# A two-layer float32 encoder on one core: projections in three 256-column products, twelve unread products at the start, and two rearranged hand-overs

## The chip, the cores and the metric

The kernel runs on one core of a Trainium2 chip. The metric is the device time of one execution in microseconds (us); smaller is better. Engines are named as the profile names them: PE (TensorE's products), PEld (its weight loads), ACT (ScalarE), DVE (VectorE), POOL (GpSimd), SP (SyncE, which issues most transfers). "L247" is line 247 of the kernel before.

## The reference, cut to what matters

```python
D_MODEL, SEQ, DEPTH, HEAD_DIM = 2048, 256, 2, 128      # one sequence of 256 tokens
N_MIX_HEADS, N_KV_HEADS, N_MEM_HEADS, N_MEM, D_FF = 12, 4, 4, 256, 8192

def reference(x, mem, ...):
    m = rms_norm(mem, mem_norm)
    h = x
    for i in range(DEPTH):
        n = rms_norm(h, attn_norm[i])
        if i == 0:      # neighbourhood attention with a bias
            q, k, v, qm = split(n @ a_w_in, [1536, 3072, 4608])
            mix = neighbourhood_attention(q, k, v, a_rpb)
        else:           # grouped-query attention, normed and rotated q and k
            q, k, v, qm = split(n @ b_w_in, [1536, 2048, 2560])
            mix = gqa_block_attention(rope(norm(q)), rope(norm(k)), v)
        km, vm = split(m @ w_mem_kv[i], 2)
        cross = memory_attention(qm, km, vm)               # 4 heads into 256 memory tokens
        h = h + concatenate([mix, cross]) @ w_o[i]
        n = rms_norm(h, mlp_norm[i])
        h = h + square(relu(n @ w_up[i])) @ w_down[i]
    return rms_norm(h, final_norm)
```

All inputs and the output are float32.

## The kernel before, in words

Every matrix is multiplied in split form: `split` (L327 to L330) makes from a float32 tile a rounded high part on ACT (L329) and the remainder, its low part, on DVE (L330). A product is then high x high, high x low and low x high, each one PE instruction, all added into one accumulator (PSUM has eight banks). Weights come from memory in chunks of 128x2048 (`raw`, 1 MB), are split in two halves of 1024 columns, and each half is one *grain* of PE work.

There are three kinds of chunk:

- **S chunks** (`s_products`, L240): one head of a projection whose result is wanted with features on partitions: `w_km0`, `w_km1`, `w_aqm` (4 chunks each), `w_aq`, `w_ak` (12 each), 36 in all, each over 16 steps of the inner dimension. The weights are stationary and the activations (`memT` or `nT`, 512 columns: 256 of high part, 256 of low part) move. A step is one product of 512 columns with the high weights (L247) and one of 256 columns with the low weights (L250), issued as two wide ones, then two narrow ones (`GROUP`). The bank holds two sums of 256 columns; `summed` (L368) adds them: a copy on ACT (L371), an addition on DVE (L373) and, for all callers, a multiplication by a row on DVE (L375).
- **M chunks** (`m_products`, L226): activations stationary, weights moving, 512 columns each, at L234, L237 and L238.
- **U chunks** (`up_grains`, `u_products`, L727): the MLP's first matrix. Weights are stationary, and a step is three products of 256 columns into one sum: high weights with both parts (L735), low weights with the high part (L736). The MLP's second matrix is done with seven accumulators `p1` to `p7` (L849 to L851).

In `begin` (L253) the first three S chunks are multiplied while the memory `memT` and their weights arrive in pieces of 256 KB; SP issues these, except the first piece of each of the three weights, which ACT issues (L142).

After that, `run_all` (L283) goes through a list of grains. Ahead of each grain it emits the load (8 grains ahead), an optional middle stage, and the split of later grains (4 ahead in the MLP); after it, a clock called `tick` goes on by one and starts what `later(n, ...)` has put off. A planner then orders the instructions of each engine by simulated times; `past` (L638) and `pin` keep instructions behind given ones.

Three places matter besides the S chunks:

- **The beginning of the MLP.** The last block of the output projection ends (`o_done`, `nb == 3`), its result is transposed into `hT`, and the first U chunks run. The split halves of U chunks are in `uh` and `ul`, two buffers each (`half_of_side`, L738), so the fourth half, grain (0, 1, 1), waits for the buffers of the second. The last block's own addition to `h`, its squares and `inv` are put off by 8, 10 and 12 ticks behind the transposes (L702 to L706).
- **The last query block's heads.** `b_q_done(blk)` starts four attention heads at ticks 1, 3, 5 and 7; each has its scores, its transposes and its values' product 3 ticks apart, and in block 2 the last of these is another tick later (`rest`). Their outputs are read by the output projection right behind.
- **The accumulators.** `sum_of` (L868) takes the seven banks of the MLP in the order p4, p3, p1, p2, p5, p7, p6.

Places in SBUF count in this program by their byte address modulo 256. In U chunks the moving data stand at 160 and the weights at 224, 64 further, but for the last step's high part, which stands at 128 (96 from the weights). In S chunks, in M chunks and in attention, both operands of a product stand at the same place.

Of the kernel before, what the change touches and what calls it, by code (L numbers as in the profile page):

```python
# [17 lines left out]
P = 128  # L18
# [17 lines left out]
GROUP = 2  # L36
# [6 lines left out]
MOVING_AT = 160  # L43

# [46 lines left out]
def encoder_kernel(ctx: ExitStack, tc: tile.TileContext, t: dict, out: bass.AP):  # L91
# [44 lines left out]
    for j in range(8):  # L136
        s = slice(j * 512, (j + 1) * 512)
        nc.sync.dma_start(mem0[:, s], t["memT"][:, s])
        if j % 2 == 0:
            s = slice(j * 256, (j + 2) * 256)  # L140
            for c in range(FIRST_CHUNKS):
                (nc.sync if j else nc.scalar).dma_start(raws[c][:, s], t["w_km0"][c][:, s])  # L142
# [11 lines left out]
    nc.scalar.activation(warm, mhalf[:, :1], AF.Exp)  # L154

# [10 lines left out]
    def halves_of(w):  # L166
# [9 lines left out]
        def prep(hf):  # L176
# [7 lines left out]
            tiles[hf] = new_half()  # L184
# [24 lines left out]
    def new_half():  # L209
        return (at.ring.tile([P, HALF], F32R, tag="hi", bufs=4, name="hi"),  # L210
                at.ring.tile([P, HALF], F32R, tag="lo", bufs=4, name="lo"))
# [28 lines left out]
    def s_products(w, k0, nk, hi, lo):  # L240

        acts, ps = w.acts(), w.ps
        for j0 in range(0, nk, GROUP):
            js = range(j0, min(j0 + GROUP, nk))
            for j in js:
                s = slice(j * P, (j + 1) * P)
                nc.tensor.matmul(ps, hi[:, s], acts[:, k0 + j, :], start=k0 + j == 0, stop=False)  # L247
            for j in js:
                s = slice(j * P, (j + 1) * P)
                nc.tensor.matmul(ps[:, SEQ:], lo[:, s], acts[:, k0 + j, :SEQ], start=False,  # L250
                                     stop=k0 + j == KT - 1)

    def begin():  # L253
# [5 lines left out]
        for q in range(4):  # L259
            for k in range(4 * q, 4 * q + 4):  # L260
                split_pair(box["memT"], mem0[:, k * SEQ : (k + 1) * SEQ], G_MEM, k)
                if k % 4 == 0:
                    for c, w in enumerate(plan[:FIRST_CHUNKS]):
                        if q % 2 == 0:
                            tiles[c] = new_half()
# [33 lines left out]
    def add_s(src, acts, done):  # L299
        def start(w):  # L300
            w.ps = at.acc.tile([P, 512], F32, tag="acc", name="ps_s")
# [66 lines left out]
    def summed(ps, name, row=None, factor=1.0):  # L368

        a = at.work.tile([P, SEQ], F32, tag="sum_a", name=f"{name}_a")  # L370
        nc.scalar.activation(a, ps[:, SEQ:], AF.Copy)  # L371
        s = at.work.tile([P, SEQ], F32, tag="sum_s", name=f"{name}_s")
        nc.vector.tensor_tensor(s, ps[:, :SEQ], a, op=ALU.add)  # L373
        if row is not None:
            nc.vector.scalar_tensor_tensor(s, s, factor, row, op0=ALU.mult, op1=ALU.mult)  # L375
# [47 lines left out]
    def attention(jobs, at, gap=1, lag=1, rest=0):  # L423

# [12 lines left out]
        for t in range(len(jobs) + 2):  # L437
            for n in range(3):
                if 0 <= t - n < len(jobs):
                    j = t - n  # L440
                    more = rest if n == 2 and j == len(jobs) - 1 else 0
                    later(at + gap * j + lag * n + more,
# [838 lines left out]
```

## Time and profile before

| | us |
|---|---|
| three runs | 2047.66, 2050.84, 2047.76 |
| median | 2047.76 |
| the profiled execution, its own time | 2048.19 |
| span of the profiled execution | 2046.4 |
| PE busy in it | 2026.7 (99%) |
| DVE busy | 1667.0 (81%) |
| ACT busy | 1251.6 (61%) |
| PE's share of the chain that ended last | 93% |

The span is from the first to the last instruction; 1.8 us of the profiled execution lie outside it. PE is busy nearly all the time, and it has 93% of the chain of waits that ended last, so the time is PE's time plus what PE waits at the start, at hand-overs and at the end. Products overlap, so the spacing from one start to the next says more than the duration of one.

### The profile page before, as it was taken

The page shows a single profiled execution, that of the slowest core. Times are in us where ns is not written, and L with a number is a line of the kernel's source. Part 1 is how long each engine was busy: PE and PEld are TensorE (multiplying, and loading weights), DVE is VectorE, ACT ScalarE, POOL GpSimd, SP SyncE. Part 2 cuts the span into 40 slices and gives each one's busy share as a digit, 9 for nine tenths or more (in the row PEclk, how much of TensorE's full clock was granted, in tenths as well). Part 3 has the DMA queues.
Part 4 walks back from the last instruction along what each step waited for, and adds up shares of the span by engine and source line. Part 5 has one row for each costly group of instructions (what it writes and reads, how often), then busy time and mean ns, then how long its engine had stood idle before and what let it go on. Part 6 is the DMA issues. An engine that isn't in the chain of part 4 may idle for free.

```text
span 2046.4 us, 31582 instructions
## 1 busy us (share of the span) xinstructions
PE 2026.7 (99%) x12516; PEld 1813.8 (89%) x12516; DVE 1667.0 (81%) x2061; ACT 1251.6 (61%) x1652; POOL 119.2 (6%) x144
## 2 busy tenths in 40 slices
PE   8999999999999999999999999999999999999998
PEld 7888888889999999999988888889999999999996
DVE  6767667558989989999897667657998989999996
ACT  6755555556666666666656557556666666666664
POOL 0000000000000000000000001000000000000000
PEclk9999999999999999999999999999999999999999
DMA  7755554727777777787775554536877777777773
GB/s 281 283 190 179 191 177 169 277 80 233 231 231 232 220 232 230 226 242 222 230 222 199 180 185 144 184 125 216 246 227 227 227 231 229 234 232 227 236 221 130
DMA packets 93429, 433.79 MB, mean 212 GB/s; under 512 B 10464, under 2 KB 12128, under 8 KB 60128
## 3 DMA queue, kind: packets, MB, share of 16 engines
q1 hardware_dynamic: 75456, 398.47, 57.3%
q0 software_dynamic: 16816, 31.46, 8.7%
q8 instruction: 98, 1.61, 0.3%
q10 hardware_dynamic: 1008, 1.84, 0.3%
q14 instruction: 51, 0.42, 0.1%
HBM read 398.17 MB, written 4.19 MB: 197 GB/s over the span
## 4 chain that ended last, share of the span: by engine, by line
PE 93%; DVE 3%; DMA 2%; issue 1%; ACT 0%; POOLq 0%; POOL 0%; SPq 0%; DVEq 0%; ACTq 0%
PE ps_u L735 21%; PE ps_u L736 11%; PE ps_m L234 8%; PE ps_m L237 8%; PE ps_m L238 8%; PE p L849 8%; PE p L850 8%; PE p L851 8%; PE ps_s L247 7%; PE ps_s L250 3%; DMA t<-in_w_pair 1%; DVE tl L330 1%; PE pt_a L410 1%; DVE ul L330 1%; PE pt_n L347 1%
## 5 line engine op out<-in xcount | busy, mean ns | idle before, releaser
L735 PE MATMUL ps_u<-hT,uh 128*128 128x256 f32 x4096 | 713.2, 278 | 0.2
L735 PEld LDWEIGHTS ps_u<-hT,uh 128*128 128x128 f32 x4096 | 627.4, 188 | 10.3 <-ACT uh L329 0.6
L736 PE MATMUL ps_u<-hT,ul 128*128 128x256 f32 x2048 | 568.9, 278 | 1.6 <-DVE ul L330 1.5
L329 ACT ACTIVATE uh<-raw_U 128x1024 fp32r<-128x1024 f32 x278 | 294.6, 1061 | 307.1 <-PE ps_u L735 290.0
L330 DVE TENSOR_TENSOR lo<-raw,hi 128x1024 fp32r<-128x1024 f32 (+1 forms) x220 | 261.4, 1194 | 164.5 <-ACT hi L329 162.9
L736 PEld LDWEIGHTS ps_u<-hT,ul 128*128 128x128 f32 x2048 | 386.2, 189 | 4.2 <-DVE ul L330 3.2
L330 DVE TENSOR_TENSOR ul<-raw_U,uh 128x1024 fp32r<-128x1024 f32 x278 | 337.3, 1218 | 40.6 <-ACT uh L329 40.5
L329 ACT ACTIVATE hi<-raw 128x1024 fp32r<-128x1024 f32 (+1 forms) x220 | 227.5, 1039 | 210.2 <-PE ps_m L238 119.1
L329 ACT ACTIVATE th<-t 128x2048 fp32r<-128x2048 f32 x112 | 215.2, 1921 | 118.7 <-PE p L851 107.8
L330 DVE TENSOR_TENSOR tl<-t,th 128x2048 fp32r<-128x2048 f32 x112 | 256.0, 2286 | 23.9 <-ACT th L329 23.5
L330 DVE TENSOR_TENSOR bl<-b,bh 128x1536 fp32r<-128x1536 f32 x112 | 196.0, 1750 | 0.3 <-ACT bh L329 0.3
L850 PE MATMUL p<-tl,a_s 128*128 128x512 f32 x448 | 174.8, 390 | 0.0
L851 PE MATMUL p<-th,a_s 128*128 128x512 f32 x448 | 174.3, 389 | 0.0
L329 ACT ACTIVATE bh<-b 128x1536 fp32r<-128x1536 f32 x112 | 166.2, 1484 | 7.3 <-PE p L851 1.2
L829 POOL DMA_DIRECT2D t<-b x112 | 97.0, 866 | 1158.8 <-DVE t L828 556.0
L849 PE MATMUL p<-th,a_s 128*128 128x512 f32 x448 | 164.1, 391 | 0.0
L247 PE MATMUL ps_s<-nT,hi 128*128 128x512 f32 x448 | 142.5, 397 | 0.0
L851 PE MATMUL p<-bh,a_s 128*128 128x512 f32 x336 | 131.1, 390 | 0.0
L850 PE MATMUL p<-bl,a_s 128*128 128x512 f32 x336 | 131.0, 390 | 0.0
L828 DVE TENSOR_TENSOR t<-t,b 128x512 f32<-128x512 f32 x112 | 77.2, 689 | 57.6 <-DMA t<-in_w_pair 46.5
L849 PE MATMUL p<-bh,a_s 128*128 128x512 f32 x336 | 108.0, 389 | 0.0
L237 PE MATMUL ps_m<-lo,nT 128*128 128x512 f32 x264 | 103.7, 393 | 0.0
(237 smaller groups left out, 3305.1 us busy)
## 6 DMA issues: line engine op xcount, KB each, us to landing
raw_U<-in_w_up SPq DMA_DIRECT2D x128, 1024.0 KB, 6.6
b<-in_w_pair SPq DMA_DIRECT2D x112, 768.0 KB, 4.5
raw<-in_w_o SPq DMA_DIRECT2D x32, 1024.0 KB, 5.0
t<-in_w_pair SPq DMA_DIRECT2D x112, 256.0 KB, 3.4
t<-b POOLq DMA_DIRECT2D x112, 256.0 KB, 6.9
raw<-in_w_b SPq DMA_DIRECT2D x21, 1024.0 KB, 4.9
raw<-in_w_av SPq DMA_DIRECT2D x12, 1024.0 KB, 4.9
raw<-in_w_aq SPq DMA_DIRECT2D x12, 1024.0 KB, 4.9
```

The lines of the kernel that those rows point to most:

```text
L234: first = nc.tensor.matmul(w.ps[i], ah, hi[:, s], start=st, stop=False)
L237: nc.tensor.matmul(w.ps[i], ah, lo[:, s], start=False, stop=False)
L238: nc.tensor.matmul(w.ps[i], al, hi[:, s], start=False, stop=sp)
L247: nc.tensor.matmul(ps, hi[:, s], acts[:, k0 + j, :], start=k0 + j == 0, stop=False)
L329: first = nc.scalar.activation(dst_hi, src, AF.Copy)
L330: return first, nc.vector.tensor_tensor(dst_lo, src, dst_hi.bitcast(F32), op=ALU.subtract)
L735: nc.tensor.matmul(ps, hi[:, s], acts[:, k, x], start=k == n == 0, stop=False)
L736: nc.tensor.matmul(ps, lo[:, s], acts[:, k, :SEQ], start=False, stop=k == KT - 1)
L829: nc.gpsimd.dma_start(s[:, 0, :], block(1), accum_op=ALU.add)
L849: nc.tensor.matmul(ps, a[:, 0, ai, :], hi[:, s], start=begins, stop=False)
L850: nc.tensor.matmul(ps, a[:, 0, ai, :], lo[:, s], start=False, stop=False)
L851: nc.tensor.matmul(ps, a[:, 1, ai, :], hi[:, s], start=False, stop=ends)
```

## The change

Five edits:

1. S chunks are multiplied as U chunks are, by one helper, `products`: each step is three products of 256 columns into one sum of 256 columns (48 products in a chunk where there were 32). The last step takes the low part first. `summed` becomes one multiplication that reads the accumulator. The split halves of S chunks start 64 bytes into buffers that are 256 bytes longer; those of M chunks stay at the start. The fourth S chunk shares the third's bank.
2. Twelve products of a 128x128 tile of ones with itself, read by nobody, stand ahead of everything on PE, and SP issues all pieces of the beginning.
3. At the MLP's beginning, grain (0, 1, 1) is split into two buffers of the tag `b` (else loads of the second matrix); the last block's addition, squares and `inv` come at ticks 6, 12 and 14, each behind the split that was traced last.
4. The seven accumulators are taken in the order p4, p7, p6, p3, p1, p2, p5.
5. In block 2 the heads start at ticks 1, 3, 4 and 6, and the last values' product is no longer put off (it comes at tick 12, where it came at 14).

The diff, cut to its core:

```diff
+STILL_AT = 64
...
-                (nc.sync if j else nc.scalar).dma_start(raws[c][:, s], t["w_km0"][c][:, s])
+                nc.sync.dma_start(raws[c][:, s], t["w_km0"][c][:, s])
...
+    idle = at.att.tile([P, P], F32, tag="att", name="idle")
+    for _ in range(12):
+        nc.tensor.matmul(idle, ones, ones, start=True, stop=True)
...
-    def new_half():
-        return (at.ring.tile([P, HALF], F32R, tag="hi", bufs=4, name="hi"),
-                at.ring.tile([P, HALF], F32R, tag="lo", bufs=4, name="lo"))
+    def new_half(kind):
+        s = slice(STILL_AT // 4, STILL_AT // 4 + HALF) if kind == "S" else slice(0, HALF)
+        return tuple(at.ring.tile([P, HALF + 64], F32R, tag=n, bufs=4, name=n)[:, s] for n in ("hi", "lo"))
...
-        acts, ps = w.acts(), w.ps
-        for j0 in range(0, nk, GROUP):
-            js = range(j0, min(j0 + GROUP, nk))
-            for j in js:
-                s = slice(j * P, (j + 1) * P)
-                nc.tensor.matmul(ps, hi[:, s], acts[:, k0 + j, :], start=k0 + j == 0, stop=False)
-            for j in js:
-                s = slice(j * P, (j + 1) * P)
-                nc.tensor.matmul(ps[:, SEQ:], lo[:, s], acts[:, k0 + j, :SEQ], start=False,
-                                     stop=k0 + j == KT - 1)
+        products(w.ps, w.acts(), k0, nk, hi, lo)
+
+    def products(ps, acts, k0, nk, hi, lo):
+
+        for j in range(nk):
+            k = k0 + j
+            s = slice(j * P, (j + 1) * P)
+            parts = (slice(0, SEQ), slice(SEQ, 512))
+            for n, x in enumerate(parts if k < KT - 1 else parts[::-1]):
+                nc.tensor.matmul(ps, hi[:, s], acts[:, k, x], start=k == n == 0, stop=False)
+            nc.tensor.matmul(ps, lo[:, s], acts[:, k, :SEQ], start=False, stop=k == KT - 1)
...
-    def add_s(src, acts, done):
+    def add_s(src, acts, done, place=None):
+
         def start(w):
-            w.ps = at.acc.tile([P, 512], F32, tag="acc", name="ps_s")
+            if place != 1:
+                box["ps_s"] = at.acc.tile([P, 512], F32, tag="acc", name="ps_s")
+            w.ps = box["ps_s"][:, (place or 0) * SEQ :][:, :SEQ]
...
-    def summed(ps, name, row=None, factor=1.0):
-
-        a = at.work.tile([P, SEQ], F32, tag="sum_a", name=f"{name}_a")
-        nc.scalar.activation(a, ps[:, SEQ:], AF.Copy)
+    def summed(ps, name, row, factor=1.0):
+
         s = at.work.tile([P, SEQ], F32, tag="sum_s", name=f"{name}_s")
-        nc.vector.tensor_tensor(s, ps[:, :SEQ], a, op=ALU.add)
-        if row is not None:
-            nc.vector.scalar_tensor_tensor(s, s, factor, row, op0=ALU.mult, op1=ALU.mult)
+        nc.vector.scalar_tensor_tensor(s, ps, factor, row, op0=ALU.mult, op1=ALU.mult)
         return s
...
-                later(8, past, add)
-                later(10, past, squares)
-                later(12, past, inv)
+                for n, fn in ((6, add), (12, squares), (14, inv)):
+                    later(n, lambda fn=fn: past(fn, box["splits"][-1]))
...
         def prep(hf):
-            own[hf] = half_of_side(own["raw"], hf)
+            if (part, m, hf) == (0, 1, 1):
+
+                own[hf] = tuple(at.side.tile([P, 3 * 512], F32R, tag="b", bufs=2, name="u_b")[:, :HALF] for _ in "hl")
+                box["splits"].append(split(*own[hf], own["raw"][:, hf * HALF :]))
+            else:
+                own[hf] = half_of_side(own["raw"], hf)
...
-            for x in ("p4", "p3", "p1", "p2", "p5", "p7", "p6"):
+            for x in ("p4", "p7", "p6", "p3", "p1", "p2", "p5"):
...
             attention([(qT[:, j, :], box["kT"][:, kv, :], None, head_of(box["vb"], kv), blk * 4 + j, box["cat"])
-                       for j, kv in enumerate(kvs)], 1, 2, 3, blk // 2)
+                       for j, kv in enumerate(kvs)], (1, 3, 4, 6) if blk == 2 else (1, 3, 5, 7), 3)
```

## The prediction

> **What bounds the kernel now.** I read the page first: the busy times and the shares of the chain.
>
> ```profile
> PE 2026.7 (99%) x12516; PEld 1813.8 (89%) x12516; DVE 1667.0 (81%) x2061; ACT 1251.6 (61%) x1652; POOL 119.2 (6%) x144
> ...
> PE 93%; DVE 3%; DMA 2%; issue 1%; ACT 0%; POOLq 0%; POOL 0%; SPq 0%; DVEq 0%; ACTq 0%
> ```
>
> PE has 93% of the chain. So a gain is either a shorter spacing of products, or one of the few holes in PE. From start to start of neighbouring products I listed each spacing over its usual value by more than 0.19 us: there are holes before 12.5, at 451 and at 1380 (both at the MLP's beginning), at 1316 (last heads), two of 0.2 at 789 and 1047, and one of 0.27 at 1324. The change touches the first four. Then the timeline of PE at each of them, first the beginning:
>
> ```profile
> 7.99 1.65 PE L247 MATMUL ps_s<-memT,hi 128*128 128x512 f32 x3 [7.99 <-DVE memT L356]
> 9.44 0.63 PE L250 MATMUL ps_s<-memT,lo 128*128 128x256 f32 x2
> 9.86 0.63 PE L247 MATMUL ps_s<-memT,hi 128*128 128x512 f32 x1
> ...
> 10.71 2.16 PE L247 MATMUL ps_s<-memT,hi 128*128 128x512 f32 x5
> 12.71 0.40 PE L250 MATMUL ps_s<-memT,lo 128*128 128x256 f32 x2
> ```
>
> Two narrow products from 9.44 to 9.86 are 0.21 us each; later they are 0.117. PE runs at half its speed until about 12.5 us. (The windows view still says clock 1.00 there: it has no record so early. The spacings decide.)
>
> The S chunks and the U chunks, once each, and U chunks where nothing else stands between them:
>
> ```profile
> 185.91 0.62 PE L247 MATMUL ps_s<-nT,hi 128*128 128x512 f32 x2
> 186.38 0.40 PE L250 MATMUL ps_s<-nT,lo 128*128 128x256 f32 x2
> 186.61 0.63 PE L247 MATMUL ps_s<-nT,hi 128*128 128x512 f32 x2
> ```
> ```profile
> 585.38 0.39 PE L735 MATMUL ps_u<-hT,uh 128*128 128x256 f32 x2
> 585.61 0.28 PE L736 MATMUL ps_u<-hT,ul 128*128 128x256 f32 x1
> 585.72 0.39 PE L735 MATMUL ps_u<-hT,uh 128*128 128x256 f32 x2
> ```
> ```profile
> 479.76 0.28 PE L736 MATMUL ps_u<-hT,ul 128*128 128x256 f32 x1
> ...
> 480.12 0.28 PE L736 MATMUL ps_u<-hT,ul 128*128 128x256 f32 x1
> ```
>
> The reader sees two S steps in 0.70 us. A step with three narrow products takes 0.34 us in one place (585.38 to 585.72) and 0.36 in another (479.76 to 480.12). The two holes:
>
> ```profile
> 451.59 0.50 PE L735 MATMUL ps_u<-hT,uh 128*128 128x256 f32 x2
> ...
> 452.84 0.39 PE L736 MATMUL ps_u<-hT,ul 128*128 128x256 f32 x1 [0.76 <-DVE ul L330]
> ```
> ```profile
> 1316.40 0.28 PE L420 MATMUL av<-pT,vb 128*128 128x256 f32 x1
> 1317.02 0.58 ACT L329 ACTIVATE pT<-pt_a 128x512 fp32r<-128x512 f32 x1
> ...
> 1317.65 0.38 PE L418 MATMUL av<-pT,vb 128*128 128x256 f32 x1 [0.97 <-ACT pT L329]
> ```
>
> **Part 1, the S chunks.** There are 36 x 16 = 576 steps. Before: the four chunks of `w_km1` begin at 55.70 and the next M product at 78.00, so 22.30 / 64 = 0.3485 us a step. After, a step is three narrow products, for which the trace has three spacings. 0.340 is the U chunk at 585 (0.1133 each), whose weights stand 64 from the data modulo 256, as the new S halves will. 0.354 is the run of U chunks from 456 to 490, at the same places: it falls into this slower spacing at a chunk's end, where two products stand 96 apart, and stays there. 0.359 is attention, operands at one place, twelve products from 153.27 to 154.70, 0.119 to 0.120 each. So the term lies between 576 x (-0.0085) = -4.9 and 576 x 0.0105 = +6.0, with 576 x 0.0055 = +3.2 for the middle row. The new S chunks keep 64 also in their last step, which speaks for the fast spacing; attention's products break in some 25 times between 100 and 340, and after such a break the U rows show both. I take half the steps at 0.340 and half at 0.354: 0.347, **-0.9 us**.
>
> The Trainium skill, page "TensorE: Matmul & The Clock Gate", section "Back-to-back issue gap", speaks against this edit: 518 cycles for 512 columns, 262 for 256, so halving a wide product costs 6 cycles, by an estimate from that page +1.4 us over 576 steps. The M chunks' wide products here, 0.227 apart, are exactly two of the fast narrow ones, so the trace puts the fixed part lower than the page; but the S chunks' own wide ones are 0.233, and that excess is what there is to win.
>
> `summed` loses 36 copies of 0.365 us on ACT (13 us) and 36 additions of 0.417 on DVE (15 us). Between 100 and 340 ACT is busy 127 and DVE 165 of 240 us and PE all 240: worth nothing. Without that cover it could not be worth more than 28 us. The shared bank and the order of the accumulators: PE has no hole at 32 or at 490, so nothing; the first accumulators used now get banks free for long, the last ones (p7 first used at 492.6) those of the last U chunks, which end at 489.6 and are read within 1 us.
>
> **Part 2, the beginning.** The slow stretch, 7.99 to 12.71, holds nine wide and four narrow products: 4.72 us; at 0.233 and 0.116 they take 2.56, so 2.16 are lost. From there to 26.95 PE has no hole, so a lead would be kept if the data come in time. Last data: the splits of `memT` end on ACT at 20.4 and DVE ends about 21.5; what PE owes then is more than 2 us, so most of the lead holds. The twelve products are float32, two passes each (the float32 product at 53.65 shows two passes of 0.215 for 256 columns, so 0.107 for 128, twice that while slow): 24 x 0.21 = 5.1 us from about 1.0, when `ones` is set, to 6.1 at the latest, before the first data are split (7.93). They cost nothing; were they late, each microsecond would cost one. The single queue puts two pieces of `memT` behind three of weights, and saves ACT 1.4 us before its table load; the second `memT` piece landed at 7.9 with the third weight piece at 8.5, all five are needed for the first quarter, so between -1.0 and +1.0, taken as 0.16 against the lead. **-2.0 us** (-3.0 to +1.0).
>
> **Part 3, the MLP's beginning, twice.** The fourth product after the one at 451.23 should start at 451.70 (0.118 each) and starts at 453.07: 1.37 us are lost, and the same at 1380. ACT's split of (0, 1, 1) begins at 450.49, when its buffer is freed; ACT is idle from 439.4 to 445.1, and in a buffer of its own the split is done there. Next late is grain (0, 2, 0): its buffer is free at 451.2, ACT and DVE need 1.05 + 1.24, so 453.6, and PE asks for it at 454.2. The addition (0.68 twice on DVE) and the squares leave this stretch; `inv` is first read at 521.8. New waits: the loads of `b`, at 382.6 and 384.7 before, now wait on SP for PE to end (0, 1, 1), about 454. Behind them are loads of U chunks; the one at 452.82 needs the buffer that (0, 1, 1) frees, which now is free before 451. Two `b` tiles are needed at 489.9, 36 us later. If a U load did fall behind, 1.6 us of wait and the shared transfer would cost up to 2 us each time. The accumulators of the last block are held some 12 us longer, leaving two banks for U chunks of 5.66 us, read within 1 us: no wait. **-2.7 us** (-2.7 to +1.3).
>
> **Part 4, the last heads.** From 1316.40 to 1317.92 PE should take 0.24 and takes 1.52: 1.28 lost, because ACT had two halves of weights to split (1315.11 to 1317.02) ahead of `pT`. The last transposes come one tick earlier, the values' product two; whether the planner puts `pT` ahead of the weights can't be seen. Half of it, **-0.6 us** (-1.3 to +1.3, one such hole more).
>
> **Sum.** -0.9 - 2.0 - 2.7 - 0.6 = -6.2. Against the profiled execution's own 2048.19 that is 2042.0; that execution lies 0.43 above the median, so 2041.6.
>
> **The rivals.** 0.2% is 4.1 us, about what a measurement of this kernel can tell from no change: faster is under 2043.7, slower over 2051.9.
>
> A, narrow products at the slow spacing throughout: for it, that U chunks in a row stay at 0.354 for seven chunks once they fall into it; against it, that the cause of the fall, the 96, is missing here. +3.2 instead of -0.9: 2045.7.
>
> B, the fast spacing holds throughout, as in most U chunks: -4.9, so 2037.6.
>
> C, a new wait takes the place of a removed one: U loads behind `b` on SP, +2 in each layer, 2045.6. For it, that SP runs its queue in order; against it, that the U load's own buffer is free earlier. An early clock that is lost again before the first data would cost only the 2.0 (2043.6) and stays within the forecast's range. The clock rule on the same page of the Trainium skill (Part 1) has PE fall back after an idle window of about 3.4 us; the gap left here is some 2 us, and no trace shows such a gap.
>
> D, slower: three weight loads a step where there were two, with PE held by the loads. The place is all S chunks; the price per product is that of the U rows just where weights change buffers, 0.122: 0.366 a step, +10.1 instead of -0.9, so 2052.6. It decides from 0.1216 a product on (9.4 us over 576 steps, 0.0163 each, on 0.3485, by three). Against it: loads (0.188 each, but 0.113 apart) keep up in every U chunk.
>
> E, the change doesn't do what it says: the planner, not the ticks, orders the engines, and (0, 1, 1) or the heads stay late: -2.9 alone, 2044.9.
>
> **How the numbers follow.** Forecast 0.42, A 0.17, B 0.20, C 0.07, D 0.09, E 0.05. Faster: forecast and B, 0.62. Same: A, C and E, 0.29. Slower 0.09. The range takes B with the better beginning (2036.6, rounded down) and A with a lost hand-over in the MLP (2045.7 + 2.7 = 2048.4): 2036.0 to 2048.5.
>
> **What would show it.** Right: products 0.117 apart from the first on, and the fourth S chunk at about 25 instead of 26.95; no hole over 0.3 us where the second U chunk begins; the hole of 1.25 us by the last `pT` smaller; S steps of 0.34 to 0.354. Wrong: S products 0.12 or more apart, which alone would undo the rest; a first product later than 8; or SP waiting on `b` with a hole in PE at the third or fourth U chunk.

## The result, and the profile after

The changed kernel took 2054.39 us (median of 12 runs, 2051.56 to 2057.97), the kernel before 2048.10 in the same comparison (12 runs, 2046.26 to 2054.25): ratio 1.0027, 95% interval [1.0018, 1.0037]. That is slower by 0.27%, and outside the predicted range. Two later comparisons (both on chip 0; the chip of the first is not known) gave the same kernel 2046.26 and 2046.42, ratio 0.9998 both times ([0.9988, 1.0007] and [0.9989, 1.0006]). So the loss is not the same in every comparison.

The page of the changed kernel, first the engines' line, then the chain that ended last, by engine:

```profile
PE 2032.2 (99%) x13116; PEld 1839.2 (90%) x13116; DVE 1654.8 (81%) x2025; ACT 1239.1 (60%) x1616; POOL 120.3 (6%) x144
...
PE 87%; DVE 6%; DMA 3%; issue 2%; ACT 1%; SPq 0%; DVEq 0%; POOLq 0%; POOL 0%; ACTq 0%
```

PE's share of the chain fell from 93% to 87%; DVE and transfers took its place. I put the first product of each stage side by side in the two profiles (product starts, in us):

| stretch | before | after | difference |
|---|---|---|---|
| start to end of the fourth S chunk | 32.52 | 30.68 | -1.84 |
| first `w_km1` chunk (55.70; 53.87) to the first U chunk (442.01; 437.75) | 386.31 | 383.88 | -2.43 |
| MLP, layer 0 (to the first product of `w_b`) | 670.48 | 678.21 | +7.73 |
| output projection of layer 1, with the last heads | 109.58 | 109.20 | -0.38 |
| MLP, layer 1 (to PE's last product) | 666.51 | 668.25 | +1.74 |

They add to +4.8, and the span went from 2046.4 to 2051.2. Both stretches ahead of the first MLP are faster, together by more than predicted (4.27 against 2.9 us); both MLPs are slower.

**Beginning.** The timeline of PE (start, duration, number behind the x):

```profile
0.98 5.49 PE L159 MATMUL idle<-ones 128*128 128x128 f32 x24 [0.98 <-POOL mhalf L153]
6.73 1.21 PE L256 MATMUL ps_s<-memT,hi 128*128 128x256 f32 x4 [0.26 <-ACT hi L338]
...
10.78 0.40 PE L256 MATMUL ps_s<-memT,hi 128*128 128x256 f32 x2
11.01 0.28 PE L257 MATMUL ps_s<-memT,lo 128*128 128x256 f32 x1
11.13 0.40 PE L256 MATMUL ps_s<-memT,hi 128*128 128x256 f32 x2
```

The last pass of the unread products starts at 6.05, the first S product at 6.73 (7.99 before), and from 7.78 to 7.90 a product takes 0.12, the full speed; at 10.78 a step takes 0.35. Before, PE ran at half its speed until 12.5. The fourth S chunk starts at 25.03 instead of 26.95.

**S chunks.** The place that the prediction showed, 185 us:

```profile
185.69 0.39 PE L256 MATMUL ps_s<-nT,hi 128*128 128x256 f32 x2
185.92 0.28 PE L257 MATMUL ps_s<-nT,lo 128*128 128x256 f32 x1
186.03 0.39 PE L256 MATMUL ps_s<-nT,hi 128*128 128x256 f32 x2
```

A step takes 0.34. The four `w_km1` chunks take 21.76 us (53.87 to 75.63) where they took 22.30.

**The MLP's beginning.** The old hole at the second U chunk is gone, and three new ones stand where the rows of PE name a releaser:

```profile
467.94 0.39 PE L257 MATMUL ps_u<-hT,ul 128*128 128x256 f32 x1 [0.68 <-DVE ul L339]
...
480.06 0.39 PE L257 MATMUL ps_u<-hT,ul 128*128 128x256 f32 x1 [0.73 <-DVE ul L339]
...
487.05 0.51 PE L256 MATMUL ps_u<-hT,uh 128*128 128x256 f32 x2 [1.30 <-ACT c L785]
```

From start to start they cost 0.84, 0.89 and 1.46 over the usual spacing, 3.2 in all; the old hole cost 1.2 by the same count. SP's own queue shows the first one's origin:

```profile
449.95 0.33 SPq L810 DMA_DIRECT2D b<-in_w_pair  x1
450.32 1.39 SPq L737 DMA_DIRECT2D raw_U<-in_w_up  x1
451.81 0.38 SPq L810 DMA_DIRECT2D b<-in_w_pair  x1
457.96 5.99 SPq L737 DMA_DIRECT2D raw_U<-in_w_up  x2
```

Both loads of `b`, which were at 382.6 and 384.7 before, now wait until grain (0, 1, 1) has released their tiles, and so stand among the U loads. The U load between them lands at 458.49, 8.2 us after its issue, the next one, issued at 457.96, at 465.46 (7.5; in the profile of before the loads from 452 to 475 take 4.8 to 5.1), and PE waits for the split of that one. The other two holes come from the work that was put off. ACT, just ahead of the third:

```profile
482.84 1.06 ACT L338 ACTIVATE uh<-raw_U 128x1024 fp32r<-128x1024 f32 x1 [0.43 <-PE ps_u L256]
483.81 1.90 ACT L338 ACTIVATE th<-t 128x2048 fp32r<-128x2048 f32 x1
485.67 1.06 ACT L338 ACTIVATE uh<-raw_U 128x1024 fp32r<-128x1024 f32 x1
486.63 0.36 ACT L785 ACTIVATE c<-ps_u 128x256 f32<-128x256 f32 x1
```

The read of a U chunk's accumulator (`c`, L785) stands in ACT's queue behind two splits of `uh` and the first split of `th`, and PE waits for that bank.

**The later parts of the MLP.** From about 690 us on `tl` (DVE's low part of the second matrix) comes late, and PE waits for it, which it did not do before. The view of waits from 690 to 1040, PE and then DVE in the changed kernel (in total, times, longest), with one of PE's waits between them:

```profile
PE p L846 <- DVE tl L339: 2.9, 6, 0.8
```
```profile
857.76 0.50 PE L846 MATMUL p<-tl,a_s 128*128 128x512 f32 x1 [0.76 <-DVE tl L339]
```
```profile
DVE t L824 <- DMA t<-in_w_pair: 29.0, 22, 3.4
```

DVE in the kernel before, the same window, where PE has no row at all:

```profile
DVE t L828 <- DMA t<-in_w_pair: 19.0, 21, 2.9
```

From 690 us to the end of layer 0, seven starts of a product that reads `tl` are 0.1 us or more over the usual spacing, 4.1 us in all; in the profile of before there is none. Behind each, the product after the wait starts some 0.1 late as well.

**The heads.** The hole behind `pT` is gone; the next is one product group later, in front of the output projection:

```profile
1321.60 0.50 PE L239 MATMUL ps_m<-hi,cat 128*128 128x512 f32 x1 [0.72 <-ACT cat L338]
```

### The profile page after: what moved, and what is told of

The parts are those of the page before. It is cut to its first block, busy times and chain, and to the rows that moved or that the text cites. A ratio compares the mean times of both kernels' runs of the same rounds, so it can differ in the third digit from the quotient of the medians.

```text
span 2051.2 us, 32668 instructions
## 1 busy us (share of the span) xinstructions
PE 2032.2 (99%) x13116; PEld 1839.2 (90%) x13116; DVE 1654.8 (81%) x2025; ACT 1239.1 (60%) x1616; POOL 120.3 (6%) x144
## 4 chain that ended last, share of the span: by engine, by line
PE 87%; DVE 6%; DMA 3%; issue 2%; ACT 1%; SPq 0%; DVEq 0%; POOLq 0%; POOL 0%; ACTq 0%
PE ps_u L256 19%; PE ps_u L257 10%; PE ps_m L239 8%; PE ps_m L242 8%; PE ps_m L243 8%; PE p L846 7%; PE p L845 7%; PE p L847 7%; PE ps_s L256 6%; PE ps_s L257 3%; DMA t<-in_w_pair 3%; DVE tl L339 2%; DVE ul L339 1%; DVE bl L339 1%; PE pt_a L415 1%
## 5 line engine op out<-in xcount | busy, mean ns | idle before, releaser
L256 PEld LDWEIGHTS ps_u<-hT,uh 128*128 128x128 f32 x4064 | 622.6, 188 | 11.1 <-ACT c L785 1.5
L339 DVE TENSOR_TENSOR ul<-raw_U,uh 128x1024 fp32r<-128x1024 f32 x276 | 335.2, 1219 | 40.5 <-ACT uh L338 40.5
L338 ACT ACTIVATE hi<-raw 128x1024 fp32r<-128x1024 f32 (+1 forms) x220 | 227.7, 1040 | 213.2 <-PE ps_m L243 123.6
L339 DVE TENSOR_TENSOR tl<-t,th 128x2048 fp32r<-128x2048 f32 x112 | 255.9, 2284 | 10.0 <-ACT th L338 10.0
L339 DVE TENSOR_TENSOR bl<-b,bh 128x1536 fp32r<-128x1536 f32 x112 | 196.1, 1751 | 2.4 <-ACT bh L338 2.4
L256 PE MATMUL ps_s<-nT,hi 128*128 128x256 f32 x896 | 158.1, 279 | 0.0
L256 PEld LDWEIGHTS ps_s<-nT,hi 128*128 128x128 f32 x896 | 137.1, 188 | 0.3
L847 PE MATMUL p<-bh,a_s 128*128 128x512 f32 x336 | 131.2, 390 | 0.0
L257 PE MATMUL ps_s<-nT,lo 128*128 128x256 f32 x448 | 124.8, 279 | 0.0
```

What stands on the lines that cost most here:

```text
L256: nc.tensor.matmul(ps, hi[:, s], acts[:, k, x], start=k == n == 0, stop=False)
L257: nc.tensor.matmul(ps, lo[:, s], acts[:, k, :SEQ], start=False, stop=k == KT - 1)
L338: first = nc.scalar.activation(dst_hi, src, AF.Copy)
L339: return first, nc.vector.tensor_tensor(dst_lo, src, dst_hi.bitcast(F32), op=ALU.subtract)
L847: nc.tensor.matmul(ps, a[:, 1, ai, :], hi[:, s], start=False, stop=ends)
```

## Experiments

Below, "`tl` ahead" is the time from the end of DVE's `tl` to the first product that reads it, its mean from 690 to 1040 us (layer 0) and from 1640 to 1960 (layer 1) in the profiled run. From 530 to 680 us its mean is 2.9 to 3.2 in every kernel but the one with POOL's addition. "Scatter" is the lowest to the highest of a kernel's runs; it grows with their number (the kernel before, with 29 to 31 runs in a comparison, has 5.4 to 8.0), so that kernels with 10 to 12 runs are compared with each other. "The S edit" is the first edit, with the shorter `summed` and the shared bank.

**First comparison: which edit loses the time?** `before_again` and `after_again` are the two kernels unchanged. `no_mlp_edit` is the changed kernel with the third edit undone, `mlp_edit_only` the kernel before with that edit alone:

```diff
-            if (part, m, hf) == (0, 1, 1):
-                own[hf] = tuple(at.side.tile([P, 3 * 512], F32R, tag="b", ...
...
-                for n, fn in ((6, add), (12, squares), (14, inv)):
-                    later(n, lambda fn=fn: past(fn, box["splits"][-1]))
+                later(8, past, add)
+                later(10, past, squares)
+                later(12, past, inv)
```

> The kernel before, profiled once more, as the measure of what differs between two executions of one program. Three theories are told apart by this run and the next three. W: all that was lost comes from the MLP's beginning (edit 3): the loads of b now come at 450 instead of 382 and delay the loads of U chunks, and ACT and DVE get the first split of the second matrix, the squares and inv in one heap. D: the later loss (from 690 us on, where tl is ready 0 to 1 us before PE asks for it instead of 3) is no work of the change, but differs from execution to execution with the transfers. K: another edit (order of the accumulators, the beginning) causes the later loss. The MLP of layer 0, from its first U product to the first product of layer 1's projection, took 670.5 us in the first profile of before and 678.2 after. W and K expect 670 to 671.5 here, D anything from 670 to 676. Ratio 1.000 in all.

> The changed kernel, profiled once more. W and K expect the MLP of layer 0 at 677 to 679 us again, with holes in PE at the same three places before 490 and with tl late after 690. D expects the three holes before 490 again, but the part after 690 anywhere between none lost and 4 us lost. Ratio to before 1.002 to 1.003 in all.

> The changed kernel with the MLP's beginning as it was before (fourth U half in uh and ul, addition, squares and inv at ticks 8, 10 and 12 behind the transposes); everything else as changed. W expects all that the other edits win and nothing lost: MLP of layer 0 at 670 to 671 us, S chunks and beginning 4 to 5 us ahead as in the first profile of after, so 2042 to 2043.5, ratio 0.997 to 0.998. K expects 2 to 4 us lost after 690 all the same: 2045 to 2047, ratio 0.999 to 1.000. D expects W's ratio in the mean, with some executions at K's.

> The kernel before with the MLP's beginning as changed, and nothing else. W expects the MLP of layer 0 at 677 to 679 us and in all 7 to 10 us lost in both layers: 2055 to 2058, ratio 1.004 to 1.005. K expects only the holes before 490 and their like in layer 1, against 2.7 us won: 2 to 4 us lost, ratio 1.001 to 1.002. My own prediction's account of this edit was 2.7 us won, ratio 0.9987, which the first profile has already refuted for the three holes but not yet for the edit by itself.

Measured, beside 2047.03 for the kernel before: `before_again` 2047.00 (0.9997 [0.9987, 1.0006]), `after_again` 2046.26 (0.9998 [0.9988, 1.0007]), `no_mlp_edit` 2045.30 (0.9987 [0.9977, 0.9997]) and `mlp_edit_only` 2046.19 (0.9996 [0.9987, 1.0005]). So the MLP edit does not lose the 6 us by itself (theory W fell): alone it gains 0.4 to 1.3 in layer 0 (669.19 against 669.62 and 670.48), by one hole of 1.0 (482.2) in place of the old. In the changed kernel its holes at 477.5 and 483.7 (1.0 and 1.6) recur. The loss behind 690 us recurred only in part: `after_again` had `tl` 2.81 ahead in layer 0 and 2.00 in layer 1, where the first profile had 0.89 and 1.55. In the profile of `no_mlp_edit` (2.08 and 2.85 ahead) nothing was lost behind 690 us. And the runs scattered: `after_again` from 2044.3 to 2050.5, `no_mlp_edit` from 2043.5 to 2049.8, `before_again` from 2046.0 to 2048.0, each with 10 runs.

**Second comparison: what makes `tl` late?** `after_third` is the changed kernel again. `edits_125` leaves out the third and fourth edit. `after_old_ticks` keeps the two `b` tiles for (0, 1, 1) and has the old three `later` lines. `after_pool_add` replaces one transfer in the changed kernel:

```diff
-            nc.gpsimd.dma_start(s[:, 0, :], block(1), accum_op=ALU.add)
+            nc.gpsimd.tensor_tensor(s[:, 0, :], s[:, 0, :], block(1), op=ALU.add)
```

> The changed kernel once more. Theory D (the loss over the two hand-overs comes from `tl` arriving late in the MLP, and how late it is differs from execution to execution with the transfers): runs scatter over 5 us or more, from about 2044 up, and the median lies anywhere from 2045 to 2054; in the profiled run layer 0 of the MLP lasts 670 us where `tl` stays 3 us ahead of its product, and up to 678 us where it is down to 0 to 1. Rival F (the loss is fixed by the program): one value again, 2046.3 within 1 us as in the last comparison or 2054 as in the first, and a scatter of 2 us.

> The changed kernel without its edits to the MLP's beginning and to the order of the accumulators. Theory K (the other order of the accumulators makes the MLP prone to the late `tl`): scatter falls from 6 us to that of the kernel before, 2 to 2.5 us, and the gains of the beginning (1.4 to 2.6), of the S chunks (2.4) and of the heads (0.4) all show: 2042 to 2043. Theory D without K: the order plays no part, since the instructions of the products' phase are the same in both; scatter 5 to 6 us and median 2044.5 to 2045.5, as with the order changed (2045.3).

> The changed kernel, with the addition, the squares and `inv` on their old ticks (8, 10, 12, and not behind the last split); the half (0, 1, 1) still takes the two `b` tiles. Theory T (the later ticks make the new holes at 477 and 483 us, since squares, `inv` and the first splits of `b` and `t` now meet on ACT and DVE): those two holes, 1.0 and 1.6 us, go, and the one at 451 does not come back; MLP layer 0 about 668.5 instead of 670.9, median 2 to 3 us under that of the changed kernel in the same comparison. Theory B (the tiles taken from `b` make them, because the first load of `b` waits for (0, 1, 1)): the holes stay within 0.3 us of their size, and the median with them.

> The changed kernel with the addition of `b` into the first quarter of `t` done by POOL as one instruction of 512 columns instead of a transfer with addition. Theory D, in which that transfer (8 us from issue to landing where it meets the load of a U chunk, and what ACT's split `th` waits for) is what makes `tl` late: `tl` is never under 1.5 us ahead of its product from 520 us on, no hole over 0.3 us in the products' phases, scatter 2.5 us, median 2042.5 to 2044.5, that is 2 us or more under the changed kernel. Rival P (the loads of `t` and `b` are late by themselves, or POOL's addition makes DVE's instructions longer): `tl` falls to 0 to 1 us as before, the scatter stays at 5 us or the time grows to 2048 or more.

Measured, beside 2047.31: `after_third` 2046.42 (0.9998 [0.9989, 1.0006], scatter 7, where rival F expected 2), `edits_125` 2046.82 (0.9995 [0.9986, 1.0004], 2043.1 to 2053.8), `after_old_ticks` 2044.98 (0.9990 [0.9981, 0.9998], 2042.8 to 2049.7) and `after_pool_add` 2079.27 (1.0148 [1.0135, 1.0162]).

The accumulators' order is not the cause (theory K fell): with the old order the profiled run, at 2053.8, had `tl` 0.83 and 0.96 ahead. But the run showed what the fourth edit is for. The S edit takes one bank fewer ahead of the MLP, and in the old order the first accumulator then gets the bank of the last U chunk:

```profile
487.13 0.50 PE L841 MATMUL p<-bh,a_s 128*128 128x512 f32 x1 [1.55 <-ACT c L781]
```

The old ticks did what theory T said: no hole of 0.3 or more over the spacing is left at the MLP's beginning in layer 0 and one of 0.4 in layer 1. Of the 3 us that this should give, 1.4 show in the median.

POOL's addition is no remedy: theory D's numbers fell, and rival P's came. `tl` was 0.50 and 0.53 ahead, because DVE itself became slower (mean ns of one behind the comma; 690 and 1219 in the changed kernel):

```profile
L339 DVE TENSOR_TENSOR ul<-raw_U,uh 128x1024 fp32r<-128x1024 f32 x276 | 373.1, 1356 | 38.9 <-ACT uh L338 38.8
...
L824 DVE TENSOR_TENSOR t<-t,b 128x512 f32<-128x512 f32 x112 | 86.3, 770 | 19.6 <-DMA t<-in_w_pair 17.8 <-DVE ul L339 1.5
```

The Trainium skill, "GPSIMD Engine Reference", section "Specifications", has POOL share DVE's path to SBUF where a DVE instruction has two inputs there; these two rows agree, by 11 to 12%. (`tl` and `bl`, which also have two inputs, kept their 2284 and 1751 ns.) What the run does show is how near DVE is to its limit: in the kernel before it is busy 72.0 of the 80 us from 600 to 680, and 75.7 of the 80 from 850 to 930. Some 80 us more on DVE came with 33 us more time than `after_third` had.

**Third comparison: which of the early edits?** `start_only` is the kernel before with the second edit alone, `s_and_heads` with the first and the fifth, `two_queues` is `after_old_ticks` with the first weight pieces on ACT's queue again, and `still_0` the changed kernel with one number changed:

```diff
-STILL_AT = 64
+STILL_AT = 0
```

> The kernel before with the edit to the beginning alone (twelve products, one load queue). Theory Q (moving five weight loads from ACT's queue to SP's, or the products ahead, disturbs the transfers of the whole program and so makes `tl` late in the MLP): scatter 5 to 7 us, median 2046 to 2048 although the beginning gains 1 to 2.6 us. Against it, theory S (the S chunks' edit makes it): scatter 2 to 2.5 us as in the kernel before, median 2045 to 2046.

> The kernel before with the narrow S products, their places and the shared bank, and with the last heads' ticks; beginning, MLP's beginning and accumulators as before. S chunks 2.4 us and heads 0.4 us gained in any theory. Theory S: scatter 5 to 7 us, median 2045 to 2047. Theory Q: scatter 2 to 2.5 us, median 2044 to 2044.6.

> The changed kernel with the old ticks of the addition, squares and `inv`, and the first weight pieces on the two load queues as before; all else as changed. Theory Q, if it is the queue: scatter 2.5 us or less, median 2042 to 2043, under every other kernel. Otherwise as with one queue (2045.0, scatter 7 us).

> The changed kernel with STILL_AT = 0: weights and data of the S products at the same place modulo 256 bytes. Theory A (the place sets the spacing, as attention's equal places go with 0.119 to 0.120): S products 0.119 to 0.120 apart, 0.358 to 0.360 a step instead of 0.3455 by the whole kernel's mean and 0.340 in the chunks of `w_km1`; these four chunks take 22.9 to 23.0 us instead of 21.76, and all S chunks 7 to 8 us more: 2053 to 2055. Rival N (256 columns take 0.1134 wherever they lie): 21.8 us and 2046.3.

Measured, beside 2047.55: `start_only` 2045.23 (0.9988 [0.9979, 0.9996], scatter 3.4), `s_and_heads` 2046.71 (0.9997 [0.9988, 1.0006], 3.8), `two_queues` 2048.22 (1.0003 [0.9994, 1.0012], 9.8) and `still_0` 2058.40 (1.0056 [1.0043, 1.0069]). The load queue is not the cause (theory Q fell): with two queues the scatter was the widest of this comparison. The beginning alone keeps its whole gain. `s_and_heads` keeps 0.8 of the 2.8 that its stages gain; 1.2 goes at 487 us, in the hole that the fourth edit avoids. Its median is the one of theory S, its scatter of 3.8 (theory S: 5 to 7) is not, and its profile lost nothing behind 690 us. It is the only run with the S edit and without the unread products.

`still_0` is the cleanest answer of the study: one number differs. Its S rows:

```profile
185.24 0.40 PE L256 MATMUL ps_s<-nT,hi 128*128 128x256 f32 x2
185.48 0.28 PE L257 MATMUL ps_s<-nT,lo 128*128 128x256 f32 x1
185.60 0.40 PE L256 MATMUL ps_s<-nT,hi 128*128 128x256 f32 x2
```

A step takes 0.36. The `w_km1` chunks take 23.02 (theory A: 22.9 to 23.0), and from there to the first U chunk 391.62 us against 383.88: 7.7 more, as theory A had it. The changed kernel had 2046.26 and 2046.42 in the comparisons before, so that `still_0` is some 12 slower; the rest lies in the two MLPs (3.5 and 2.0 us longer than in the profile of `after_third`), with `tl` 1.38 and 1.64 ahead. It also reaches the MLP later than the kernel before (445.8 against 442.0), so that late `tl` does not need a PE that is early.

**Fourth comparison: PE's own code?** PE's instructions are loaded in packets of 16 KB: 98 of them for 12516 products with their weight loads, 102 for 13116, one per 256 instructions. In the trace of before, in the later parts of the MLP, loads of `t` that meet one take 3.98 us on average and the others 3.67, additions into `t` 7.07 and 5.67. But a longer transfer meets a packet more often by chance alone: with the packets moved by up to 10 us in time, the same count gives differences of 0.2 and 0.8 on average (-0.4 to 0.8, and -0.1 to 1.4), so that a cost of the packets is not shown. The change shifts where in the loop they fall. `code_back` (on `after_old_ticks`), `after_code_back` (on the changed kernel), `code_moved` (on `start_only`) and `code_round` (on `after_old_ticks`) add 20, 20, 32 and 64 products ahead:

```diff
+    for _ in range(20):
+        nc.tensor.matmul(idle[:, :16], ones, ones[:, :16], start=True, stop=True)
```

> The changed kernel with the old ticks (2045.0 us and a scatter of 7 us before) and 20 more products of no use, of 16 columns, behind the twelve: 40 products and 40 weight loads more, so that PE's code in the MLP lies where it lay in the kernel before, modulo the 256 instructions of one code load. Theory L (the places of the code loads against the loads of `b` and `t` make `tl` late): from 690 to 1040 us and from 1640 to 1960 `tl` is on average 2.4 us or more ahead of its product, as in the kernel before, instead of 0.9 to 2.0; scatter 3.5 us or less; median 2042 to 2043 plus what the longer row of products costs the beginning (0 to 3 us, read from the first chunk of `w_km1`). Theory N (the code has no part in it): `tl` 1 to 2 us ahead, scatter 6 us or more, median 2045 plus the beginning's cost.

> The changed kernel itself with the same 20 products. Theory L: `tl` 2.4 us or more ahead in the later parts, scatter 3.5 us or less, median 2043 to 2044 plus the beginning's cost. Theory N: as the changed kernel, 2046.4 plus that cost, scatter 6 us or more.

> The kernel before with the edit to the beginning alone (2045.2 us, scatter 3.4 us) and 32 more products of no use, so that PE's code lies where it lies in the changed kernel, modulo one code load. No S edit, no edit to the MLP. Theory L: `tl` falls to 0.9 to 2.0 us ahead in the later parts, scatter 6 us or more, and the median rises by 2 us or more over 2045.2 and over what the beginning loses (up to 4 us). Theory N: `tl` 2.4 us ahead, scatter 3.5 us, median 2045.2 plus the beginning's loss.

> The changed kernel with the old ticks and 64 more products of no use: 256 instructions, one whole code load, so that the places in the MLP stay those of the changed kernel. Theory L: as without them, `tl` 1 to 2 us ahead, scatter 6 us or more, median 2045 plus the beginning's loss (up to 8 us). If products of no use or a later beginning help by themselves: `tl` 2.4 us or more ahead and a scatter of 3.5 us, as in code_back.

Measured, beside 2048.29: `code_back` 2051.16 (1.0014 [1.0004, 1.0024], scatter 11), `after_code_back` 2056.03 (1.0035 [1.0023, 1.0047]), `code_moved` 2056.33 (1.0037 [1.0025, 1.0049], scatter 1.2 in five runs) and `code_round` 2068.45 (1.0096 [1.0083, 1.0109]). Theory L fell on both sides. `code_moved`, with PE's code where the changed kernel has it, kept `tl` 2.93 and 2.82 ahead: it starts its first `w_km1` chunk 10.65 us later than `start_only` and is 11.1 slower (in another comparison), so that it loses little else. `after_code_back`, with the code put back, had 1.55 and 0.83, and `code_back`, where layer 0 had 2.58 as theory L wanted, 2.08 in layer 1 and the scatter of theory N. `code_round` had 2.44 and 2.61 and a scatter of 3.4 in four runs: that is what its expectation gave for the other case, that products of no use or a later beginning help by themselves. Its beginning loses 22.95 us beside `after_old_ticks` (not up to 8), nearly its whole distance from the 2045 expected. Whether so late a beginning helps was not followed up; the smaller delays of `code_back`, `after_code_back` and `still_0` did not.

**Fifth comparison: is the S edit needed?** `no_s` has the second and the fifth edit, and (0, 1, 1) in the `b` tiles with the old ticks; S chunks, `summed` and the accumulators' order are those of before. `code_dve` is `after_old_ticks` with two instructions that nobody reads, so that ACT and DVE have as many as before:

```diff
+        a = at.work.tile([P, SEQ], F32, tag="sum_a", name=f"{name}_a")
+        nc.scalar.activation(a, ps, AF.Copy)
+        nc.vector.tensor_tensor(a, ps, a, op=ALU.add)
```

> The kernel before with the edits to the beginning and to the last heads and with the half (0, 1, 1) in the two `b` tiles, old ticks; S chunks, shared bank, `summed` and the accumulators' order as before. Theory S (the S chunks' edit brings the later `tl`): `tl` on average 2.4 us or more ahead in the later parts, scatter 3.5 us or less, and the gains show: beginning 1.9, (0, 1, 1) 1.2 in each layer, heads 0.4, so 2042 to 2043. Rival E (whatever brings PE earlier to the MLP brings it): `tl` 1 to 2 us ahead, scatter 6 us or more, 2044.5 to 2046.

> The changed kernel with the old ticks, and in `summed` one copy of 256 columns on ACT and one addition on DVE that nobody reads: as many instructions on these two engines as in the kernel before. Theory V (the loads of ACT's and DVE's code fall elsewhere and make `tl` late): `tl` 2.4 us or more ahead, scatter 3.5 us or less, 2041.5 to 2043. If the S edit acts in another way, or not at all: as without these instructions, 2045.0, scatter 6 us or more.

Measured, beside 2047.47: `no_s` 2042.90 (0.9977 [0.9968, 0.9986], 2041.7 to 2045.1), `code_dve` 2047.36 (0.9995 [0.9984, 1.0006], 2041.8 to 2054.5). `no_s` has the lead, the scatter (3.3) and the median that theory S gave; theory V fell. `no_s` also has the lowest time of the study. Its page and its waits on DVE from 690 to 1040:

```profile
PE 2028.3 (99%) x12540; PEld 1815.9 (89%) x12540; DVE 1668.3 (82%) x2061; ACT 1253.0 (61%) x1652; POOL 120.3 (6%) x144
...
PE 98%; DMA 1%; ACT 0%; issue 0%; DVE 0%; SPq 0%; POOLq 0%; POOL 0%; ACTq 0%
```
```profile
DVE t L835 <- DMA t<-in_w_pair: 12.7, 16, 1.8
```

All kernels but the one with POOL's addition, by whether they have the S edit (`tl` ahead in us, layer 0 / layer 1; one profiled execution each, which is the fastest run of `s_and_heads` and the slowest of `edits_125`):

| without the S edit | | with it | |
|---|---|---|---|
| before | 2.46 / 2.68 | after | 0.89 / 1.55 |
| before_again | 2.93 / 3.08 | after_again | 2.81 / 2.00 |
| mlp_edit_only | 2.97 / 3.04 | after_third | 1.98 / 2.71 |
| start_only | 2.41 / 2.95 | no_mlp_edit | 2.08 / 2.85 |
| code_moved | 2.93 / 2.82 | edits_125 | 0.83 / 0.96 |
| no_s | 2.94 / 2.97 | after_old_ticks | 1.85 / 1.15 |
| | | two_queues | 1.85 / 1.33 |
| | | s_and_heads | 2.06 / 2.53 |
| | | still_0 | 1.38 / 1.64 |
| | | code_back | 2.58 / 2.08 |
| | | after_code_back | 1.55 / 0.83 |
| | | code_round | 2.44 / 2.61 |
| | | code_dve | 1.68 / 1.73 |

On the left every value is 2.4 or more; on the right 19 of 26 are below that.

The same traces show what it costs. I take the time from the product of `tl` next to 690 us to the end of layer 0, and from the one at the same place of layer 1 to PE's end, beside the first profile of before. Without the S edit no kernel takes longer (0 to -0.9 us for both layers together). With it, nine of 13 lose 1.0 to 10.0 us; `after_third`, `no_mlp_edit`, `s_and_heads` and `code_round` lose nothing, and their mean leads are 1.98 or more in both layers. The runs point the same way: the middle half of a kernel's runs (10 runs or more) spans 0.7 to 2.1 us in the other kernels without the S edit, 0.7 to 3.1 in the six comparisons' runs of the kernel before, 2.2 to 4.9 in those with the S edit, and 1.6 in `s_and_heads`.

**What stays open.** That late `tl` comes, in most profiles, with the S edit and the unread products together, that it goes when the S edit is left out (`no_s`), and how it costs time, is shown. Whether the S edit does it by itself is not: `s_and_heads`, without the unread products, lost nothing there, and no run has the S edit alone. By what it acts 350 us and more later is open too. From 521 to 1106 us the order of instructions on each engine is the same before and after, and in the programs as built the MLP's tiles stand at the same places in SBUF. Accumulators' order, load queue, MLP edit, place of PE's code and number of ACT's and DVE's instructions were each put back (some together with the old ticks) and did not mend it. The parts of the S edit (narrow products, 256 bytes more per half, shared bank, shorter `summed`) were not run one by one; of the last, only the number of instructions was put back, by `code_dve`. Nor is it known why the changed kernel lost 6.3 us in the first comparison and nothing in two others: `after_code_back` lost 7.7 on chip 10, of which its later beginning is 1.3, and no run settles whether the chip makes the difference.

## Why the prediction was wrong, point by point

- **S chunks, -0.9 forecast, -2.43 measured** behind the beginning. The mechanism and both spacings were right (0.340, and 0.354 after a break), only their shares were not: I took half and half. Of the spacings inside S chunks some two in three were fast, so that a step has 0.3445 on average, and 576 x (0.3445 - 0.3485) is -2.3. The prediction held two products 96 bytes apart to be what makes PE fall into the slower spacing; S chunks have none, and a third of their spacings were still 0.116 to 0.120; the two longest slow runs, from 222.6 and from 296.2 us, begin right behind an M chunk. Rival D (0.122 a product) did not occur. By the figures of the Trainium skill ("TensorE: Matmul & The Clock Gate", "Back-to-back issue gap": 518 cycles for 512 columns, 262 for 256) splitting a wide product costs an estimated 6 cycles. The four `w_km1` chunks gained 0.54 us: here the measurement decides. The wide products of before stood at one place with their weights, which costs narrow ones 0.006 to 0.007 each (`still_0`); no run has wide products with their weights 64 bytes further.
- **Beginning, -2.0 forecast:** -1.84, -2.65 and -0.91 in three profiles of the changed kernel. Right in size and kind, with a spread that I had bounded by -3.0 to +1.0. In the last of the three the early clock was lost again (last section), which the prediction had named and priced in rival C.
- **MLP's beginning, -1.4 each forecast.** Here a step failed: that the addition and the squares "leave this stretch" was taken as free, and so was "no wait" for the banks. They meet the first splits of `b`, `t` and U chunks on ACT and DVE at 472 to 490 us, with holes of 0.9 and 1.5. The old ticks took both holes away in layer 0. "U loads behind `b` on SP", which was rival C at 2 us in each layer, occurred in layer 0 of the first profile with 0.84, and not in the other two.
- **Last heads, -0.6 forecast, -0.38 measured.** The hole of 1.28 by `pT` went as planned, and one of 0.9 in front of the output projection came. The prediction halved the gain; the row behind `pT` on ACT, the split of `cat`, would have told it what is late next.
- **`summed` "worth nothing", shared bank and accumulators' order "so nothing".** No row ahead of the MLP speaks against that. But the shared bank shifts all later banks by one, and without the fourth edit that costs 1.2 to 1.7 us at the first product; the prediction looked at each bank's use in the new order only.
- **What had no term at all** is what decided, and it is the main step that failed: the prediction took it that what is won ahead of the MLP's later parts is kept through them, and put them at nothing without a row for it. They cost 5.8 of the 7.73 us lost in layer 0; up to 690 us the changed kernel had lost 1.9, about the 3.2 of new holes less the 1.2 of the old. The prediction itself had two holes in these parts, of 0.2 at 789 and 1047, and passed over them ("The change touches the first four"). They say that DVE's hand-overs are at their limit there: both stand in front of a product that reads `ul`, and the lead of `tl`, 2.6 to 3.3 us up to 680, is 0.1 at 786 in the profile of before. What made the lead shrink further stays open, as said above. A range that holds such a stage should have been wider on the slow side: 2036.0 to 2048.5 left no place for it.

## What to carry to other kernels

Where a second engine is 95% busy and only a few tenths ahead, a gain anywhere on the first engine is not safe: list the smallest lead of each hand-over, not the holes alone, and look at the spread of the runs (their middle half, or as many runs of each kernel) as at the median, for it shows a lead that is used up in some executions. An edit that moves work off a critical stretch needs a row for the place that it goes to. And when several edits come together, try them with one left out at a time: the fastest kernel here leaves out the S edit and keeps the old ticks and the old order of accumulators.

## What the runs showed of the hardware that was not expected

- **Place decides the spacing.** In S chunks, narrow products with the weights 64 bytes from the data modulo 256 go 0.1133 apart at best, with both at one place 0.119 to 0.120 (21.76 against 23.02 us for 192 products), with nothing else changed. Other distances were not tried there.
- **The clock can be lost in 2 us.** In `after_third` the unread products had reached full speed (0.112 a pass, from 3.9 us on), then came 2.1 us from the start of the last of them to the first S product, 1.87 of them idle, and PE was at half its speed again:

```profile
0.98 4.31 PE L159 MATMUL idle<-ones 128*128 128x128 f32 x24 [0.98 <-POOL mhalf L153]
7.16 1.50 PE L256 MATMUL ps_s<-memT,hi 128*128 128x256 f32 x4 [1.87 <-ACT hi L338]
8.46 0.41 PE L257 MATMUL ps_s<-memT,lo 128*128 128x256 f32 x1
8.67 0.63 PE L256 MATMUL ps_s<-memT,hi 128*128 128x256 f32 x2
```

  0.21 from 8.46 to 8.67 is a narrow product at half speed. In `no_mlp_edit` it was lost over gaps of 0.8 and 1.3 us with two products between them. After single gaps of 1.3 and 1.4 us (`edits_125`, `no_s`) it stayed at full speed. The Trainium skill ("TensorE: Matmul & The Clock Gate", "Part 1: The HAM clock gate") has the clock fall after an idle window of about 3.4 us; a shorter gap was enough here.
